# Output projection of a hybrid attention block: halves by kind of head, another order of the products, other banks

## The chip, the cores and the metric

The kernel runs on one core of a Trainium2 chip. The metric is the device time of one execution in microseconds (us); the median of several runs is compared.

## What is computed

One layer of a streaming encoder: a combined input projection, 16 heads of attention (8 stick-breaking, 8 forgetting), an output projection with a residual, a squared-ReLU MLP with a residual, a final norm. 512 tokens, width 2048, all in float32. The change touches the line with `w_out`:

```python
mixed = jnp.concatenate([head_rmsnorm(o_sb, g_out_sb[l]),
                         head_rmsnorm(o_fox, g_out_fox[l])], axis=-1)
x = x + jnp.einsum('bse,ed->bsd', mixed, w_out[l])

h2 = rmsnorm(x, g_mlp[l])
u = jax.nn.relu(jnp.einsum('bsd,df->bsf', h2, w_up[l]))
x = x + jnp.einsum('bsf,fd->bsd', u * u, w_down[l])
```

`mixed` has 16 heads of 128 columns: heads 0 to 7 are stick-breaking, 8 to 15 forgetting.

## The kernel before

Every float32 product is three fp32r matmuls on TensorE (`mm3`, lines 76 to 79): high by high, high by low, low by high. An operand is split by a cast on ScalarE (line 59, the high part) and a subtraction on VectorE (line 60, the low part).

The large products are Strassen-Winograd products: both operands are halved along both dimensions, 7 products of sums of quarters take the place of 8, and some products accumulate on others. The **output projection** (in the trace some 576 to 760 us) does this for two blocks of columns, `db` 0 and 1. Its left operand is `mixed`, halved along the tokens and along the heads: before, one half holds the even heads and the other the odd ones (`(m s)`: head 2m+s), so that a sum joins heads 2m and 2m+1, m = 0 to 7. `g_form(p, ...)` makes the split operand `G[p]` of product p for some m, in rooms of two halves (high and low) named by `ROOMS`. The row sums of `mixed` that the products need are made in place by VectorE (`a_source`, lines 1231 to 1239). The right operand, sums of quarters of `w_out`, comes ready from DRAM (`wraws`, `wsums`, `whigh`, made earlier by `WeightSums`) or is split on arrival.

A product is four pieces (`out_piece(p, db, m0)`, m0 = 0, 2, 4, 6; each two m). A piece is 12 matmuls of 128x512, so a product is 48. It accumulates in a PSUM tile of two banks, `[P, 2, NT]`; there are three, `accoa`, `accob`, `accoc`, called A, B, C. For db 0 the products 1, 6, 7, 4 follow one another in A (6 goes on where 1 ended, so 1 must be read out before 6 begins), 2 is in B, 5 and 3 in C; for db 1 A and B change places. The order of the products is 1, 2, 6, 5, 7, 3, 4.

Behind each product, `take(p, db)` adds the banks to a quarter of the residual x on VectorE (line 1453, one instruction of 128x1024, for product 4 two of 128x512); the quarters are loaded by `begin` (line 1447, 512 KB on SyncE's queue). When a quarter is whole, `turn_quarter` transposes it for the MLP: 8 transposes of 128x128 on TensorE (line 1460), two in a PSUM tile, copies with the norm's weight on ScalarE, and the quarter is written to DRAM. From the turned quarters `left_form` makes the left operands of the next stage. Pending left forms are taken up one by one behind pieces.

The heads end in the order forgetting 6, 7, 0 to 5, then stick-breaking 0 to 7. Stick-breaking 6 and 7 are the last; the pieces and sums with them come last in the stage's first products (m = 3 before).

The instructions of this stage are not ordered by hand: a scheduler orders each engine's queue from the program's dependences and its own durations; `issue_after` lines bind an instruction behind another. The weights' pieces rotate through three rooms (`hi_lo`), with a fourth (`px`) until product 5 of db 0.

Of the kernel before, what the change touches and what calls it, by code (L numbers as in the profile page):

```python
# [15 lines left out]
P = 128  # L16
# [21 lines left out]
def block_kernel(ctx, tc, x, g_attn, w_in, b_f, g_out_sb, g_out_fox, w_out, g_mlp, w_up, w_down, g_final, y):  # L38
# [676 lines left out]
    with tc.tile_pool(name="att", bufs=1, side="right", reuse_waits="tile") as at, \  # L715
# [259 lines left out]
        class WeightSums:  # L975
# [415 lines left out]
    A, B = (A, B), (B, A)  # L1391
    S_OF = xp.tile([P, NH, 2 * P], F32, tag="hr1", name="s12")
    out_rows = w_out.rearrange("(m s p) c -> s p m c", s=2, p=P)
# [12 lines left out]
    def out_piece(p, db, m0):  # L1406

        hi, lo = (w.rearrange("p (a b) -> p a b", a=2) for w in hi_lo(2 * NT))
        if db == 0 and p in (1, 2):
            begun_ = [sp.dma_start(w.bitcast(F32), wraws[p - 1][:, m0 // 2, i]) for i, w in enumerate((hi, lo))][1]  # L1410
        elif db == 0 and p == 6:
            begun_ = sp.dma_start(hi.bitcast(F32), whigh[:, m0 // 2])
            sp.dma_start(lo.bitcast(F32), wsums[:, m0 // 2, 3, db])
        else:
            raw = out_weights(p, db, m0)
            casts[0] = split(hi, lo, raw[0])
            begun_ = raw[1]
        ps = {2: B[db], 5: C, 3: C}.get(p, A[db])
        for t in range(2):
            ts = slice(t * P, (t + 1) * P)  # L1420
            for i in range(2):
                mm3(ps[:, t, :], G[p][0][:, m0 + i, ts], G[p][1][:, m0 + i, ts], hi[:, i, :], lo[:, i, :],
                    m0 + i == 4 and p in (1, 5, 2), m0 + i == 3)
        return begun_
# [15 lines left out]
    def begin(t, j, db):  # L1440

        if t + j + db == 0:

            quarter[t, j] = wp.tile([P, 2, NT], F32, tag="wraw", name="x2")
        else:
            quarter[t, j] = xp.tile([P, 2, NT], F32, tag="x2", name="x2", bufs=3)
        sp.dma_start(quarter[t, j], xq[:, 2 * t:2 * t + 2, (2 * j + db) * NT:(2 * j + db + 1) * NT])

    def take(p, db):
        q, ps = {1: ((0, 0), A[db]), 5: ((1, 1), C), 6: ((0, 1), A[db]), 2: ((0, 0), B[db]), 7: ((1, 1), A[db]),  # L1450
                 3: ((0, 1), C), 4: ((1, 0), A[db])}[p]
        for t in range(2) if p == 4 else [slice(0, 2)]:
            dve.tensor_tensor(quarter[q][:, t, :], quarter[q][:, t, :], ps[:, t, :], op=ALU.add)
# [40 lines left out]
    pending = []  # L1494
    for db in range(2):
        if db == 1:
            begin(0, 0, db)
        else:

            for p in (1, 2):  # L1500
                g_form(p, (4, 8), (0, 2), (2, 3))
            with tc.issue_after(last_heads[2].ins):
                for p in (4, 5):
                    g_form(p, (4, 8), (0, 2), (2, 3))
            more_parts.append(lambda: parts_at(px, "px"))
            out_piece(1, 0, 4)
            with tc.issue_after(last_heads[3].ins):
                out_piece(1, 0, 6)
            with tc.issue_after(last_heads[2].ins):
                with tc.issue_after(last_heads[0].ins):  # L1510
                    out_piece(1, 0, 0)
                    out_piece(2, 0, 4)
                with tc.issue_after(last_heads[1].ins):
                    out_piece(2, 0, 6)
                    out_piece(2, 0, 0)
            begin(0, 0, db)
            for p in (1, 2, 4, 5):
                g_form(p, (3, 4))
            g_form(6, (4, 6), (6, 8), (0, 2), (2, 4))
            last_heads[4] = lows[0]  # L1520
        for i, p in enumerate(G_ORDER):
            for m0 in (2,) if db == 0 and p in (1, 2) else (4, 6, 0, 2):
                ins = out_piece(p, db, m0)
                if pending:
# [3 lines left out]
                if (db or p in (3, 4)) and m0 in (6, 2) and first_loads:  # L1528
# [4 lines left out]
                if db == 0 and p in (6, 5, 7) and m0 == 2:  # L1533
# [3 lines left out]
                if db == 0 and p in (6, 5) and m0 != 4:  # L1537

                    with tc.issue_after(last_heads[4].ins):
                        g_form({6: 7, 5: 3}[p], {6: (4, 8), 0: (0, 2), 2: (2, 4)}[m0])  # L1540
# [6 lines left out]
            if db == 1 and p == 2:  # L1547
# [5 lines left out]
            if db == 1:  # L1553
                pending += [(q, 0, j) for q in A_ORDER[2 * i:2 * i + 2] for j in range(2)]
# [10 lines left out]
            if db == 1 and p == 3:  # L1565
                left_form(1, 1, 1)
                for j in range(2):
                    left_form(2, 1, j)
                for q in (4, 5, 6):
                    left_form(q, 1, 1)  # L1570
# [7 lines left out]
        else:  # L1578
            turn_quarter(1, 0, db)
# [583 lines left out]
```

## Time and profile before

| | us |
|---|---|
| median of 3 runs | 2004.07 |
| lowest, highest | 2003.90, 2004.32 |
| the profiled execution's span | 2002.0 |
| TensorE busy in it | 1993.2 |
| VectorE busy | 1745.6 |
| ScalarE busy | 1202.3 |

The span is measured from the first to the last instruction of the profiled execution; the runs' times are 2.07 longer by the median. PE is TensorE, DVE VectorE, ACT ScalarE, SP SyncE, whose queue issues the transfers. A matmul row shows a duration that overlaps with the next row's, since matmuls are pipelined; the pace is read from the starts.

### The profile page before, as it was taken

How to read it: one execution, taken by the hardware profiler on the slowest of the kernel's cores; microseconds unless marked ns; L12 is line 12 of the kernel's file. 1: busy time of each engine (PE TensorE's matmuls, PEld its weight loads, DVE VectorE, ACT ScalarE, POOL GpSimd, SP SyncE). 2: the span in 40 equal slices, each digit the busy share in tenths (PEclk: the TensorE clock that was granted, in tenths of full speed). 3: DMA queues.
4: the chain of work that ended last, by engine and by line, in shares of the span. 5: the costliest groups of instructions: out<-in, count | busy, mean ns of one | idle time of the engine just before them, and what ended most of it. 6: DMA issues, size and time to landing. Idle time of an engine off the chain costs nothing.

```text
span 2002.0 us, 27075 instructions
## 1 busy us (share of the span) xinstructions
PE 1993.2 (100%) x10288; PEld 1727.1 (86%) x10288; DVE 1745.6 (87%) x1997; ACT 1202.3 (60%) x1648; POOL 63.3 (3%) x73
## 2 busy tenths in 40 slices
PE   9999999999999999999999999999999999999998
PEld 9998888888898889888888888888888888888887
DVE  7886888888878678999999999998798888988896
ACT  7544766787765566767676776766543444344344
POOL 0000011010110000000000000000000000000003
PEclk9999999999999999999999999999999999999999
DMA  7417977777668962666766666666694674674642
GB/s 262 157 65 246 292 230 212 227 225 219 212 214 279 299 221 95 200 203 199 219 184 215 199 203 201 199 211 233 245 348 165 228 279 142 239 262 171 215 163 85
DMA packets 309570, 423.54 MB, mean 212 GB/s; under 512 B 49424, under 2 KB 205376, under 8 KB 302912
## 3 DMA queue, kind: packets, MB, share of 16 engines
q1 hardware_dynamic: 308688, 419.71, 63.9%
q10 hardware_dynamic: 752, 2.11, 0.3%
q8 instruction: 81, 1.33, 0.3%
q14 instruction: 49, 0.40, 0.1%
HBM read 315.45 MB, written 96.49 MB: 206 GB/s over the span
## 4 chain that ended last, share of the span: by engine, by line
PE 100%; DVE 0%; issue 0%; DVEq 0%; ACT 0%; ACTq 0%
PE psa L1313 11%; PE accd L79 8%; PE accd L77 8%; PE accd L78 8%; PE accq L77 6%; PE accq L78 6%; PE accq L79 6%; PE psa L1311 6%; PE psc L1313 5%; PE psc L1311 3%; PE psb L1313 3%; PE psb L1311 1%; PE m L79 1%; PE m L77 1%; PE m L78 1%; PE accoa L77 1%
## 5 line engine op out<-in xcount | busy, mean ns | idle before, releaser
L1949 ACT CAST wh<-wd 128x1024 fp32r<-128x1024 f32 x126 | 125.0, 998 | 168.2 <-PE accd L79 55.3
L1835 DVE TENSOR_TENSOR wl<-wu,wh 128x1024 fp32r<-128x1024 f32 x158 | 192.6, 1219 | 12.2 <-ACT wh L1829 12.0
L77 PE MATMUL accq<-hH,wh 128*128 128x512 f32 x512 | 200.3, 391 | 0.0
L78 PE MATMUL accq<-hL,wh 128*128 128x512 f32 x512 | 199.4, 389 | 0.0
L79 PE MATMUL accq<-hH,wl 128*128 128x512 f32 x512 | 199.4, 389 | 0.0
L1829 ACT CAST wh<-wu 128x1024 fp32r<-128x1024 f32 x158 | 167.6, 1061 | 44.0 <-issue 27.9
L1313 PE MATMUL psa<-f,wh 128*128 128x512 f32 x720 | 179.0, 391 | 0.0
L79 PE MATMUL accd<-wh,uf 128*128 128x512 f32 x436 | 169.6, 389 | 0.0
L78 PE MATMUL accd<-wl,uf 128*128 128x512 f32 x436 | 169.6, 389 | 0.0
L77 PE MATMUL accd<-wh,uf 128*128 128x512 f32 x436 | 169.5, 389 | 0.0
L1313 PEld LDWEIGHTS psa<-f,wh 128*128 128x128 f32 x720 | 132.3, 188 | 25.6
L1956 DVE TENSOR_TENSOR wl<-wd,wh 128x1024 fp32r<-128x1024 f32 x126 | 143.9, 1150 | 10.6 <-ACT wh L1949 10.6
L1949 ACT CAST wx<-wd 128x1024 fp32r<-128x1024 f32 (+1 forms) x82 | 80.8, 994 | 107.4 <-PE accd L79 43.6
L1670 DVE TENSOR_TENSOR m<-m,accd 128x1024 f32<-128x1024 f32 x84 | 102.1, 1216 | 47.9 <-PE accd L79 47.9
L79 PEld LDWEIGHTS accq<-hH,wl 128*128 128x128 f32 x512 | 96.1, 188 | 20.3
L77 PEld LDWEIGHTS accq<-hH,wh 128*128 128x128 f32 x512 | 96.2, 188 | 19.0
L78 PEld LDWEIGHTS accq<-hL,wh 128*128 128x128 f32 x512 | 96.2, 188 | 18.9
L77 PE MATMUL accd<-wx,uf 128*128 128x512 f32 x284 | 110.5, 389 | 0.0
L78 PE MATMUL accd<-wx,uf 128*128 128x512 f32 x284 | 110.5, 389 | 0.0
L79 PE MATMUL accd<-wx,uf 128*128 128x512 f32 x284 | 110.5, 389 | 0.0
L1311 PEld LDWEIGHTS psa<-f,wl 128*128 128x128 f32 x720 | 96.0, 191 | 5.4
L1311 PE MATMUL psa<-f,wl 128*128 128x256 f32 x720 | 98.3, 282 | 0.0
(464 smaller groups left out, 5120.5 us busy)
## 6 DMA issues: line engine op xcount, KB each, us to landing
wu<-in_w_up_dram SPq DMA_DIRECT2D x60, 1024.0 KB, 6.5
ufd<-st SPq DMA_DIRECT2D x98, 512.0 KB, 4.2
wd<-in_w_down_dram SPq DMA_DIRECT2D x48, 1024.0 KB, 8.4
uf<-ufd SPq DMA_DIRECT2D x42, 1024.0 KB, 7.5
wraw<-in_w_in_dram SPq DMA_DIRECT2D x68, 512.0 KB, 5.7
wo<-wsums SPq DMA_DIRECT2D x28, 512.0 KB, 4.7
q<-in_w_in_dram SPq DMA_DIRECT2D x32, 384.0 KB, 5.3
wd<-in_w_down_dram SPq DMA_DIRECT2D x16, 768.0 KB, 5.8
```

Of the source, the lines that this page charges most:

```text
L77: pe.matmul(out, sh, mh, start=first, stop=False, skip_group_check=True)
L78: pe.matmul(out, sh, ml, start=False, stop=False, skip_group_check=True)
L79: return pe.matmul(out, sl, mh, start=False, stop=last, skip_group_check=True)
L1311: ins = pe.matmul(ps[:, 2 * P:], lo[:, a, :], f_parts(p, a)[0], start=False, stop=last, skip_group_check=True)
L1313: ins = pe.matmul(ps, hi[:, a, :], f_both(p, a), start=a == PAIRS[0] and p in (1, 5), stop=last, skip_group_check=True)
L1670: dve.tensor_tensor(M[p][:, :, db, :], M[p][:, :, db, :], ps, op=ALU.add)
L1829: act.copy(rooms[k][0], srcs[k])
L1835: lows[0] = dve.tensor_tensor(lo, srcs.pop(k), hi.bitcast(F32), op=ALU.subtract)
L1949: act.copy(rooms[k + 3][0], srcs[k + 3])
L1956: dve.tensor_tensor(rooms[k + 2][1], srcs.pop(k + 2), rooms[k + 2][0].bitcast(F32), op=ALU.subtract)
```

## The change

Six things change in the output projection. (1) `mixed` and `w_out` are halved as `(s m)`: one half is the stick-breaking heads, the other the forgetting ones, and a sum joins heads m and m + 8. The last heads are then m = 6 and 7, and the pieces go in the order m0 = 0, 2, 4, 6. (2) Product 2 of db 0 and product 2 of db 1 come first; then product 1 of db 0, and 6, 5, 7, 3, 4; for db 1 1, 6, 5, 7, 3, 4. (3) The banks: product 2 in A (db 0) and B (db 1), the chain 1, 6, 7, 4 in C (db 0) and B (db 1), 5 and 3 in A (db 0) and C (db 1). (4) The residual quarter (0, 0) of db 1 is loaded at the start of the stage and kept, in the room `ROOMS[1]`, where the low half of product 2's operand lies before. (5) A turn is put on a list and made behind the first piece of the next product. (6) Left forms of db 1's partner operands are listed at other products.

```diff
@@ WeightSums.load
-                    src = w_out[(2 * self.m + s) * P:(2 * self.m + s + 1) * P].rearrange("p (j c) -> p j c", j=2)
+                    src = w_out[(s * NH + self.m) * P:(s * NH + self.m + 1) * P].rearrange("p (j c) -> p j c", j=2)
...
-    G_ORDER = (1, 2, 6, 5, 7, 3, 4)
+    G_ORDER = (1, 6, 5, 7, 3, 4)
     G = {p: [form.tile([P, NH, 2 * P], F32R, tag=ROOMS[2 * i + c], name=f"g{p}") for c in range(2)]
-         for i, p in enumerate(G_ORDER)}
+         for i, p in enumerate((2, 1, 6, 5, 7, 3, 4))}
...
-    A, B = (A, B), (B, A)
+    firsts, chains, sides = (A, B), (C, B), (A, C)
...
-            a_form(p, mixed[:, 2 * m0:2 * m1].rearrange("p (m s) n -> p m s n", s=2), [g[:, m0:m1, :] for g in G[p]])
+            a_form(p, mixed_halves[:, m0:m1], [g[:, m0:m1, :] for g in G[p]])
...
-        ps = {2: B[db], 5: C, 3: C}.get(p, A[db])
+        ps = {2: firsts[db], 5: sides[db], 3: sides[db]}.get(p, chains[db])
...
+        elif t + j == 0:
+            quarter[t, j] = form.tile([P, 2, NT], F32, tag=ROOMS[1], name="x2")
...
             g_form(2, (0, 4), (4, 8))
             g_form(1, (0, 4), (4, 6))
...
+                    for m0 in (0, 2, 4, 6):
+                        out_piece(2, 1, m0)
+                    for m0 in (0, 2, 4):
+                        out_piece(1, 0, m0)
+            begin(0, 0, 1)
+            kept = quarter[0, 0]
+            take(2, 1)
+            begin(0, 0, 0)
+            take(2, 0)
+            for p in (1, 5):
+                g_form(p, (6, 7), (7, 8))
+            g_form(6, (0, 4), (4, 6), (6, 8))
...
+        for p in G_ORDER:
+            for m0 in (6,) if db == 0 and p == 1 else (0, 2, 4, 6):
                 ins = out_piece(p, db, m0)
+                if m0 == 0 and to_turn:
+                    with tc.issue_after(ins.ins):
+                        turn_quarter(*to_turn.pop())
...
             if db == 1:
-                pending += [(q, 0, j) for q in A_ORDER[2 * i:2 * i + 2] for j in range(2)]
+                pending += [(q, 0, j) for q in {1: (4, 5, 6), 6: (2, 7), 5: (3,)}.get(p, ()) for j in range(2)]
...
-            if p in (2, 7, 3):
-                turn_quarter(*{2: (0, 0), 7: (1, 1), 3: (0, 1)}[p], db)
+            if p in (1, 7, 3):
+                to_turn.append(({1: (0, 0), 7: (1, 1), 3: (0, 1)}[p]) + (db,))
```

In the excerpts of the queues below a row is line, operation, output and inputs with the number of the tile, shape, and what the instruction waits for (queues of transfers, DVE, Activation, PE).

TensorE's queue of the kernel before, at the end of product 2 of db 0 and the start of product 6:

```order
L77 MATMUL accob_5600<-wh_5767,g2_5565 128x512
L78 MATMUL accob_5600<-wl_5768,g2_5565 128x512
L79 MATMUL accob_5600<-wh_5767,g2_5566 128x512
L77 MATMUL accoa_5599<-wx_5800,g6_5567 128x512 [waits DMAHW0_49,DVE_49,Activation_49]
L78 MATMUL accoa_5599<-wx_5800,g6_5567 128x512 [waits DMAHW1_49]
L79 MATMUL accoa_5599<-wx_5800,g6_5568 128x512 [waits DVE_49]
```

The same of the kernel after, at the end of product 1 of db 0 and the start of product 6:

```order
L77 MATMUL accoc_5601<-wh_5830,g1_5565 128x512
L78 MATMUL accoc_5601<-wl_5831,g1_5565 128x512
L79 MATMUL accoc_5601<-wh_5830,g1_5566 128x512
L77 MATMUL accoc_5601<-wx_5847,g6_5567 128x512 [waits DMAHW5_49,DVE_49,Activation_49]
L78 MATMUL accoc_5601<-wx_5847,g6_5567 128x512 [waits DMAHW6_49]
L79 MATMUL accoc_5601<-wx_5847,g6_5568 128x512
```

Before, product 6 in accoa begins behind product 2 in accob; after, it begins in the bank in which the matmul ahead of it, the last of product 1, is.

VectorE's queue before, in the same place (x2 is a residual quarter, g1 to g7 the operands' low halves, ph a head's norm, wx a weight's split):

```order
L969 SCALAR_TENSOR_TENSOR mixed_1750<-os_last_5528,g_rest_78,ph_5530 128x512 [waits DVE_49]
L60 TENSOR_TENSOR g2_5566<-mixed_1750,g2_5565 128x256 [waits Activation_49]
L60 TENSOR_TENSOR g4_5576<-mixed_1750,g4_5575 128x256 [waits Activation_49]
L1453 TENSOR_TENSOR x2_5727<-x2_5727,accoa_5599 128x1024 [waits DMAHW5_49,PE_49]
L60 TENSOR_TENSOR g6_5568<-mixed_1750,g6_5567 128x512 [waits Activation_49]
L1233 TENSOR_TENSOR mixed_1750<-mixed_1750 128x256 [waits DVE_49]
L60 TENSOR_TENSOR g6_5568<-mixed_1750,g6_5567 128x512 [waits Activation_49] x2
L1453 TENSOR_TENSOR x2_5727<-x2_5727,accob_5600 128x1024 [waits DVE_49,PE_49]
L60 TENSOR_TENSOR g5_5570<-mixed_1750,g5_5569 128x256 [waits Activation_49]
L1235 TENSOR_TENSOR mixed_1750<-mixed_1750 128x2x256 [waits DVE_49]
L60 TENSOR_TENSOR wx_5877<-wo_5878,wx_5877 128x1024 [waits DMAHW6_49,DMAHW1_49,DMAHW7_49,DMAHW0_49,Activation_49]
```

After, up to the addition of product 1 of db 0, the last row:

```order
L60 TENSOR_TENSOR g6_5568<-mixed_1750,g6_5567 128x1024 [waits PE_49,Activation_49]
L60 TENSOR_TENSOR g6_5568<-mixed_1750,g6_5567 128x512 [waits Activation_49]
L60 TENSOR_TENSOR g5_5570<-mixed_1750,g5_5569 128x256 [waits Activation_49]
L1233 TENSOR_TENSOR mixed_1750<-mixed_1750 128x2x256 [waits DVE_49]
L1454 TENSOR_TENSOR x2_5805<-x2_5805,accob_5600 128x1024 [waits DMAHW3_49,PE_49]
L60 TENSOR_TENSOR g6_5568<-mixed_1750,g6_5567 128x512 [waits Activation_49]
L1235 TENSOR_TENSOR mixed_1750<-mixed_1750 128x4x256
L1235 TENSOR_TENSOR mixed_1750<-mixed_1750 128x2x256 x2
L1237 TENSOR_TENSOR mixed_1750<-mixed_1750 128x4x256
L1237 TENSOR_TENSOR mixed_1750<-mixed_1750 128x2x256 x2
L60 TENSOR_TENSOR g7_5572<-mixed_1750,g7_5571 128x1024 [waits Activation_49]
L1454 TENSOR_TENSOR x2_5808<-x2_5808,accoc_5601 128x1024 [waits PE_49]
```

The addition of accob, product 2 of db 1, to the kept quarter x2_5805 stands there, ahead of the sums for g7 and of the addition of accoc.

SyncE's queue before, at the weights of products 1, 2 and 6 of db 0:

```order
L1410 DMA wl_5751<-wraws1_93 128x1024 [waits DMAHW4_49,PE_49]
L1410 DMA wh_5750<-wraws1_93 128x1024 [waits DMAHW5_49,PE_49]
L1410 DMA wl_5768<-wraws2_94 128x1024 [waits DMAHW6_49,DMAHW0_49,PE_49]
L1410 DMA wh_5767<-wraws2_94 128x1024 [waits DMAHW7_49,DMAHW1_49,PE_49]
L1412 DMA wx_5800<-whigh_92 128x1024 [waits PE_49]
L1413 DMA wx_5800<-wsums_86 128x1024
L1413 DMA wl_5816<-wsums_86 128x1024 [waits DMAHW2_49,PE_49]
```

After:

```order
L1409 DMA wl_5790<-wraws1_93 128x1024 [waits PE_49]
L1409 DMA wh_5789<-wraws1_93 128x1024 [waits DMAHW1_49,PE_49]
L1409 DMA wl_5831<-wraws1_93 128x1024 [waits DMAHW2_49,PE_49]
L1448 DMA x2_5805<-in_x_dram 128x2x512 [waits DMAHW3_49,PE_49]
L1409 DMA wh_5830<-wraws1_93 128x1024 [waits DMAHW4_49]
L1411 DMA wx_5847<-whigh_92 128x1024 [waits DMAHW5_49,PE_49]
L1412 DMA wx_5847<-wsums_86 128x1024 [waits DMAHW6_49]
```

The load of the kept quarter stands between the two halves of the last weights of product 1, and waits for PE.

## Rows read from the trace of the kernel before

**Rows 1.** The page: busy time of engines, granted clock, chain of work.

```profile
PE 1993.2 (100%) x10288; PEld 1727.1 (86%) x10288; DVE 1745.6 (87%) x1997; ACT 1202.3 (60%) x1648; POOL 63.3 (3%) x73
...
PE 100%; DVE 0%; issue 0%; DVEq 0%; ACT 0%; ACTq 0%
```

**Rows 2.** PE's waits: line waited for, us in total, times, longest.

```profile
PE vx L305 <- DVE still L301: 1.6, 1, 1.6
```

**Rows 3.** Windows: length, busy us of PE, PEld, DVE, ACT, POOL; clock, DMA.

```profile
620.00:770.00 150.00, 150.00 (x757) 127.40 (x756) 113.31 (x122) 91.22 (x145) 0.00 (x0) 1.00 0.71 231
```

**Rows 4.** Timeline of PE (start, us, line, out<-in), where the bank changes.

```profile
660.96 0.39 PE L77 MATMUL accoc<-wh,g 128*128 128x512 f32 x1
...
661.41 0.39 PE L79 MATMUL accoc<-wh,g 128*128 128x512 f32 x1
661.64 0.39 PE L77 MATMUL accoa<-wh,g 128*128 128x512 f32 x1
```

**Rows 5.** Timeline of PE at a turn.

```profile
655.27 0.40 PE L77 MATMUL accoc<-wh,g 128*128 128x512 f32 x1
655.51 1.04 PE L1460 MATMUL tr<-ident,x 128*128 128x128 f32 x8
...
656.61 0.39 PE L79 MATMUL accoc<-wh,g 128*128 128x512 f32 x1
```

**Rows 6.** Timeline of DVE at two takes; in brackets idle time before, and its releaser.

```profile
661.84 1.22 DVE L1453 TENSOR_TENSOR x<-x,accoc 128x1024 f32<-128x1024 f32 x1 [0.41 <-PE accoc L79]
...
685.40 1.22 DVE L1453 TENSOR_TENSOR x<-x,accob 128x1024 f32<-128x1024 f32 x1 [0.18 <-PE accob L79]
```

**Rows 7.** Timeline of PE at the first piece of product 2.

```profile
605.24 0.39 PE L77 MATMUL accob<-wx,g 128*128 128x512 f32 x1
```

**Rows 8.** Timeline of DVE: the first sum g4, and instructions of each size in a row.

```profile
595.09 2.15 DVE L60 TENSOR_TENSOR g<-mixed,g 128x1024 fp32r<-128x1024 f32 x3
...
603.43 0.68 DVE L1235 TENSOR_TENSOR mixed<-mixed 128x512 f32<-128x512 f32 x1
604.03 0.41 DVE L60 TENSOR_TENSOR g<-mixed,g 128x256 fp32r<-128x256 f32 x1
604.37 1.28 DVE L1235 TENSOR_TENSOR mixed<-mixed 128x512 f32<-128x512 f32 x2
...
607.10 0.69 DVE L967 TENSOR_TENSOR n<-n,ra 128x512 f32<-128x512 f32 x1
607.83 0.69 DVE L968 SCALAR_TENSOR_TENSOR n<-n,ra 128x512 f32<-128x512 f32 x1
...
631.16 1.21 DVE L60 TENSOR_TENSOR g<-mixed,g 128x1024 fp32r<-128x1024 f32 x1
632.30 1.22 DVE L60 TENSOR_TENSOR wl<-wo,wh 128x1024 fp32r<-128x1024 f32 x1
```

**Rows 9.** Timeline of DVE where it stood idle in this stretch, and at product 1's take.

```profile
606.38 0.69 DVE L966 SCALAR_TENSOR_TENSOR n<-ssq,ra 128x512 f32<-128x512 f32 x1 [0.72 <-ACT ra L961]
...
612.83 0.76 DVE L60 TENSOR_TENSOR g<-mixed,g 128x256 fp32r<-128x256 f32 x2 [0.47 <-ACT g L59]
614.28 1.22 DVE L1453 TENSOR_TENSOR x<-x,accoa 128x1024 f32<-128x1024 f32 x1 [0.70 <-PE accoa L79]
```

**Rows 10.** The residual's tiles (x) in 560 to 770: their transfers, issue to landing.

```profile
DMA to landing us min/median/max: 4.3/5.2/7.8
```

**Rows 11.** PE's last matmul, and windows behind them (clock behind POOL's column).

```profile
1994.47 0.28 PE L79 MATMUL acce<-ws,us 128*128 128x256 f32 x1
...
1996.50:1997.00 0.50, 0.00 (x0) 0.00 (x0) 0.50 (x3) 0.41 (x2) 0.00 (x0) 1.00 0.00 0
1997.00:1997.50 0.50, 0.00 (x0) 0.00 (x0) 0.50 (x2) 0.50 (x2) 0.00 (x0) 0.53 0.00 0
```

**Rows 12.** Timeline of PE at the start of the kernel.

```profile
1.58 1.65 PE L305 MATMUL vx<-still 128*128 128x256 f32 x6 [1.58 <-DVE still L301]
...
7.62 0.40 PE L311 MATMUL vz<-wl,hH 128*128 128x264 f32 x2
```

More of the change, by code (lines that the diff above doesn't have):

```diff
@@ L1422, in out_piece @@
                 mm3(ps[:, t, :], G[p][0][:, m0 + i, ts], G[p][1][:, m0 + i, ts], hi[:, i, :], lo[:, i, :],
-                    m0 + i == 4 and p in (1, 5, 2), m0 + i == 3)
+                    m0 + i == 0 and p in (1, 5, 2), m0 + i == NH - 1)
         return begun_
@@ L1492, in left_form @@
         a_form(p, hr[db][j], [F[p][db][:, 2 * j:2 * j + 2, c, :] for c in range(2)])
-    pending = []
+    pending, kept, to_turn = [], None, []
     for db in range(2):
         if db == 1:
-            begin(0, 0, db)
-        else:
-            for p in (1, 2):
-                g_form(p, (4, 8), (0, 2), (2, 3))
+            quarter[0, 0] = kept
+            pending += [(1, 0, j) for j in (1, 0)]
+        else:
+            g_form(2, (0, 4), (4, 8))
+            g_form(1, (0, 4), (4, 6))
             with tc.issue_after(last_heads[2].ins):
-                for p in (4, 5):
-                    g_form(p, (4, 8), (0, 2), (2, 3))
+                g_form(4, (0, 4), (4, 8))
+                g_form(5, (0, 4), (4, 6))
@@ L1520, in block_kernel @@
+            g_form(6, (0, 4), (4, 6), (6, 8))
             last_heads[4] = lows[0]
-        for i, p in enumerate(G_ORDER):
-            for m0 in (2,) if db == 0 and p in (1, 2) else (4, 6, 0, 2):
+        for p in G_ORDER:
+            for m0 in (6,) if db == 0 and p == 1 else (0, 2, 4, 6):
                 ins = out_piece(p, db, m0)
+                if m0 == 0 and to_turn:
+                    with tc.issue_after(ins.ins):
+                        turn_quarter(*to_turn.pop())
+                    if db == 1 and p == 4:
+                        left_form(1, 1, 1)
+                        for j in range(2):
+                            left_form(2, 1, j)
+                        for q in (4, 5, 6):
+                            left_form(q, 1, 1)
@@ L1527, in block_kernel @@
                         left_form(*pending.pop(0))
-                if (db or p in (3, 4)) and m0 in (6, 2) and first_loads:
+                if (db or p in (3, 4)) and m0 in (2, 6) and first_loads:
                     with tc.issue_after(ins.ins):
@@ L1532, in block_kernel @@
                         units[u].load(k, a)
-                if db == 0 and p in (6, 5, 7) and m0 == 2:
+                if db == 0 and p in (6, 5, 7) and m0 == 6:
                     with tc.issue_after(ins.ins):
                         begin(*{6: (0, 1), 5: (1, 1), 7: (1, 0)}[p], db)
-                if db == 0 and p in (6, 5) and m0 != 4:
+                if db == 0 and p in (6, 5) and m0 != 0:
                     with tc.issue_after(last_heads[4].ins):
-                        g_form({6: 7, 5: 3}[p], {6: (4, 8), 0: (0, 2), 2: (2, 4)}[m0])
+                        g_form({6: 7, 5: 3}[p], {2: (0, 4), 4: (4, 6), 6: (6, 8)}[m0])
             if db == 0 and p == 5:
@@ L1546, in block_kernel @@
                 units += [Unit(0), Unit(1)]
-            if db == 1 and p == 2:
+            if db == 1 and p == 1:
                 begin(0, 1, db)
@@ L1560, in block_kernel @@
                     take_squares()
-            if p in (2, 7, 3):
-                turn_quarter(*{2: (0, 0), 7: (1, 1), 3: (0, 1)}[p], db)
+            if p in (1, 7, 3):
+                to_turn.append(({1: (0, 0), 7: (1, 1), 3: (0, 1)}[p]) + (db,))
             if db == 1 and p == 6:
                 left_form(1, 1, 0)
[L1565 to L1570, printed above, removed]
         if db == 1:
@@ L1578, in block_kernel @@
         else:
-            turn_quarter(1, 0, db)
+            to_turn.append((1, 0, db))
     ops.close()
```

19 lines of the change are left out of this document (7 added, 12 removed).

## The prediction

> **What bounds the kernel now.** I read the page first. TensorE is busy for 1993.2 us of a span of 2002.0, and the chain of work that ended last is put down to PE at 100% [rows 1]. The list of waits then has one entry for PE, 1.6 us at the very start [rows 2], and in a stretch that holds most of the output projection (620 to 770 us) PE is busy in 150.00 of 150 us and at full clock, while VectorE has 113.31 [rows 3]. So PE alone sets the end. A change that leaves the number of matmuls as it is can win only gaps of PE, and it loses whatever new wait it puts into PE's queue. The order confirms that the products are the same: 14 products (7 for each column block db) of 48 matmuls 128x512.
>
> What can be won? A matmul follows the last every 0.2266 us, also where the bank changes [rows 4]. The only places in the stage where this pace breaks are the turns of the residual: 8 transposes between two matmuls, as the one at 655.51 [rows 5]. A transpose has a quarter of the columns, so 0.057 us by the same pace, and 8 of them 0.45. From the matmul ahead (655.27) to the second behind (656.61) there are 1.34 us, of which 0.45 + 2 x 0.227 are due: a loss of 0.43. Eight turns lose 3.5. **A gain is bounded by about 3.5 us**, and only if all transposes leave the place between matmuls, which the change does not do.
>
> **The change, part by part.**
>
> *Turns behind a piece.* Before, the turns stood 25 matmuls into a following product already (so by the order; the one at 655.51 is in accoc's product [rows 5]). Now they are hung behind the first piece (12 matmuls) of the next product, and the scheduler puts most of them where they stood. Value 0; bounds -0.3 to 0.2, half of one turn's loss to either side, rounded.
>
> *Halves by kind of head and product 2 first.* The sums of heads are now head k plus or minus head k+8. The pieces that need the heads finished last (stick-breaking 6 and 7) are the last of each product, so product 1 of db 0 now needs them only in its last piece, at 624.3 by the count below, where before that product was whole and read out at 614.28 [rows 9]. Both product 2s (96 matmuls) run without them. I looked whether that cover is needed: PE waits for nothing there now, so its worth is 0. What it costs is in the queues. Four weight splits of 128x1024 on VectorE and one take (the addition of a bank to the residual) for product 2 of db 1 come ahead of db 0's other products instead of behind them, into the stretch where VectorE still has the last heads' norms and the sums g6 and g7.
>
> *Banks.* Product 6 continues to accumulate on product 1's bank (it needs 1+6), so its first matmul must wait until VectorE has read product 1 out. Before, product 2 stood between the two, in another bank: 48 x 0.2266 = 10.9 us in which the take was hidden. Now 6 follows 1 in the same bank with nothing between, in both column blocks; the order shows a wait for DVE on that first matmul, and the take itself as one instruction for both banks. This is a new wait on the only engine that matters. Its bare price: the last matmul of a product starts at 661.41, the take at 661.84 (0.43 later, after 0.41 of idle time, so VectorE was ready), and lasts 1.22 [rows 6]. With about 0.1 for the signal back (no row shows it; 0 to 0.3), less the 0.23 that the next matmul would take anyway: 0.43 + 1.22 + 0.1 - 0.23 = **1.5 us** for each of the two, if VectorE stands ready.
>
> *Is VectorE ready at the first one?* PE first. The first piece of product 2 begins at 605.24 before [rows 7]; up to there PE has done 48 matmuls of the first two products (36 of product 1, 12 of 2; in the new order all 48 of product 2), so in the new one product 2 of db 1 begins there. Behind it come 96 matmuls until product 1 ends: last matmul 605.24 + 95 x 0.2266 = 626.77, take possible at 627.2, product 6 due at 627.0. Now VectorE. From the first sum g4 (595.09 [rows 8]) up to the take the new order has 15 instructions of 128x1024, 12 of 128x512, 6 of 128x256 and 8 of the norm chain. One follows another by 1.14, 0.60, 0.35 and 0.71 [rows 8]: 17.1 + 7.2 + 2.1 + 5.7 = 32.1 us, so it reaches the take at 627.2 if it never waits. There is no slack, and every wait of VectorE before this point lengthens PE's stall. Such waits:
> - for ScalarE's casts. Before, VectorE lost 0.72 and 0.47 at two such places [rows 9]. In the new order two stand out: a sum behind the rooms it is written to, and g6, queued on ScalarE behind the cast for the last head. I take 0.3 + 0.75 = 1.05; bounds 0.3 to 1.6.
> - for the residual quarter of db 1. Its load goes to the room in which the low half of product 2's operand lies, so SyncE may issue it only when PE has ended product 2 of db 1: 605.24 + 48 x 0.2266 = 616.1, with drain and issue 616.9 to 617.2. The transfers of x in this stretch, its loads and its writes, take 4.3 to 7.8 us from issue to landing, 5.2 by the median [rows 10]; I use 4.5 to 6.1, some 0.8 around it: landed 621.6 to 623.2. VectorE reaches the addition that needs it 6.4 us of work and that addition's 1.14 ahead of the take, at 619.6, with the waits above about 621.0. Wait 0.6 to 2.2; queued behind it are a sum g6, six sums for the next products, g7 and the take for which PE stands. The load also stands ahead of product 1's last weights on SyncE, which would land near 622 and are wanted at 624.3, and so cost nothing.
> - 0.2 for the take of db 0's product 2, which waits for PE.
>
> Together 1.8 to 3.4. The **first stall** is then 1.5 + (1.8 to 3.4) = 3.3 to 4.9; I take 4.1.
>
> *The second stall* (db 1, seven products later, near 700). The take of 685.40 waited 0.18 for PE and so was reached at 685.22 [rows 6]; VectorE arrives just in time there. 1.5; bounds 1.4 to 2.2.
>
> *VectorE in db 1's products 6 and 5* has more splits and left forms ahead of the weights' due times; by my count the margins are 0.8, 0.25 and 0.2 us at three pieces. 0.2; bounds 0 to 0.6.
>
> **Sum:** 4.1 + 1.5 + 0.2 = +5.8 on a span of 2002.0. The median of the runs, 2004.07, is 2.07 above the profiled span, which I carry over: 2002.0 + 5.8 + 2.07 = **2009.9**. By the bounds (3.3 + 1.4 + 0 - 0.3 = 4.4 and 4.9 + 2.2 + 0.6 + 0.2 = 7.9) this case reaches from 2008.5 to 2012.0.
>
> **The rivals.**
>
> *The clock falls in the first stall.* [...] PE then resumes at half pace: at the start of the kernel six matmuls 128x256 last 1.65 us, or 0.27 each, against 0.113 by the pace of [rows 4] for half the columns; two of 128x264 in 0.40 at 7.62 are about full pace again [rows 12]. Some 5 us at half pace lose about 2.5, a part of that 1.7. Time 2009.9 + 1.7 to 2.5 = 2011.6 to 2012.4, with the stall's spread of 0.8 up to 2013.2. Against it: one place at the end shows the fall, and a PE that merely stands between two full-rate stretches is not in this trace. [...]
>
> *VectorE is ready after all (the side that is not slower).* If the casts cost nothing and the quarter lands before VectorE comes to it, it reaches the take at 627.2, and only the two bare waits stay: 2 x 1.5 = +3.0, that is 2007.1. It decides from the point where 1.8 us of waits vanish. For it: my count adds up the queue in the order printed, and a duration 2% shorter over 32 us gives back 0.6; before, VectorE had idle time in this stretch [rows 9]. Against it: the load's issue is tied to PE, and 4.3 us is the quickest transfer [rows 10].
>
> *The wait is not there.* If product 6's first matmul waited only for an older event, or the take were early, the sum would be near 0 to +1: 2004 to 2005. The order speaks against it, since the bank's chain needs the readout.
>
> *A gain.* Turn gaps closed and no stall: at best 2000.5. Nothing in the order shows it.
>
> **How the numbers follow.** Forecast 0.42 (2009.9). Clock falls 0.31 (2011.6 to 2013.2). VectorE ready 0.17 (2007.1). Wait not there 0.07 (2004.5). Gain 0.03. From below, leaving out the last two (0.10) brings the low end to 2006.7, 0.4 under the third; the high end takes in the clock's case to 2013.2 and leaves out under 0.1. 0.2% of 2004.07, about what a measurement of this kernel can tell from no change, is 4.0 us: 2000.1 to 2008.1. Faster: the 0.03 of a gain. Same: 0.17 + 0.07, less a little of the former's upper end: 0.22. Slower: 0.75.
>
> **What would show it.** Right: in the list of waits of the changed kernel two entries of PE for DVE, of 3 to 5 us near 627 and about 1.5 near 700, both at the first matmul of product 6 and behind the take; VectorE busy without idle from about 621 up to it, with an idle of 0.6 to 2.2 before the addition of the kept quarter, released by a DMA. A granted clock under 1.00 behind 627 is the second case. Two stalls of 1.5 are the third. Wrong would be: no wait of PE at a first matmul of product 6; a stall elsewhere (the weights of product 1's last piece, the last heads); a PE stall of over 6 us; or turns that lose much less than 0.43 each.

## The result, and the profile after

The changed kernel takes 2011.79 us (median of 5 runs, 2011.61 to 2012.32) against 2004.06 (5 runs, 2003.90 to 2004.32): 7.73 us more, a ratio of 1.0039 with a 95% interval of 1.0027 to 1.0052. It is slower, by 0.4%. The time lies in the predicted range (2006.7 to 2013.2), but the forecast's own case (2009.9) is not the one that occurred: it is the second, in which the clock falls.

The list of PE's waits in the profile after (line waited for, us in total, times, longest), which answers to [rows 2], has two new entries, both at the first matmul of product 6, which follows product 1 in the same bank with the read-out between them (a hand-over, below). "Issue" on the first means that the profile names no releaser; the rows of VectorE below name it.

```profile
PE accoc L77 <- issue: 4.3, 1, 4.3
...
PE accob L77 <- DVE x L1454: 1.4, 1, 1.4
```

The timeline of PE after at these two places and at a short wait ahead of the first, where product 1's last weights are late (start, us, line, out<-in, in brackets the idle time before and its releaser):

```profile
624.09 0.39 PE L79 MATMUL accoc<-wh,g 128*128 128x512 f32 x1
624.56 0.47 PE L77 MATMUL accoc<-wh,g 128*128 128x512 f32 x1
...
627.16 0.39 PE L79 MATMUL accoc<-wh,g 128*128 128x512 f32 x1
631.88 0.77 PE L77 MATMUL accoc<-wx,g 128*128 128x512 f32 x1 [4.33 <-issue]
632.44 0.63 PE L78 MATMUL accoc<-wx,g 128*128 128x512 f32 x1
632.87 0.63 PE L79 MATMUL accoc<-wx,g 128*128 128x512 f32 x1
...
635.33 0.39 PE L79 MATMUL accoc<-wx,g 128*128 128x512 f32 x1
...
702.23 0.39 PE L79 MATMUL accob<-wh,g 128*128 128x512 f32 x1
704.02 0.47 PE L77 MATMUL accob<-wh,g 128*128 128x512 f32 x1 [1.41 <-DVE x L1454]
```

Product 1 ends with the matmul at 627.16, product 6 begins at 631.88 instead of 627.39: 4.49 us. Of its first eight matmuls six are 0.43 apart where [rows 4] has 0.2266; from 635.33 on the pace is 0.23 to 0.24 again. Set against the due time those eight lose 1.6. The second hand-over, 702.23 to 704.02, loses 1.56. The late weights at 624.56 lose 0.33, the matmul behind included (this trace names no releaser there; two of the runs below name the weights' transfer). Together 4.49 + 1.6 + 1.56 + 0.33 = 8.0; the span grew from 2002.0 to 2010.1, by 8.1. Nothing else in the stage breaks the pace but the eight turns, which cost what they did.

VectorE after, from the addition of product 2 of db 1 to that of product 1 of db 0 (same columns):

```profile
617.77 2.16 DVE L60 TENSOR_TENSOR g<-mixed,g 128x1024 fp32r<-128x1024 f32 x3 [0.53 <-ACT g L59]
619.97 0.69 DVE L1233 TENSOR_TENSOR mixed<-mixed 128x512 f32<-128x512 f32 x1
623.01 1.22 DVE L1454 TENSOR_TENSOR x<-x,accob 128x1024 f32<-128x1024 f32 x1 [2.35 <-DMA x<-in_x_dram]
624.15 0.68 DVE L60 TENSOR_TENSOR g<-mixed,g 128x512 fp32r<-128x512 f32 x1
624.75 2.42 DVE L1235 TENSOR_TENSOR mixed<-mixed 128x1024 f32<-128x1024 f32 x3
627.09 2.42 DVE L1237 TENSOR_TENSOR mixed<-mixed 128x1024 f32<-128x1024 f32 x3
629.43 1.22 DVE L60 TENSOR_TENSOR g<-mixed,g 128x1024 fp32r<-128x1024 f32 x1
630.56 1.21 DVE L1454 TENSOR_TENSOR x<-x,accoc 128x1024 f32<-128x1024 f32 x1
```

The reader is to see three things. VectorE stands for 2.35 us for the load of the kept quarter. From 623.01 it works without a pause for 7.6 us, on things that PE does not need yet, while PE stands from 627.4. The addition that PE needs comes last, at 630.56, and 1.3 us later PE goes on.

Windows of after (length, busy us of PE, PEld, DVE, ACT, POOL, then the granted clock, DMA share, GB/s):

```profile
616.50:623.00 6.50, 6.50 (x31) 5.37 (x30) 3.58 (x6) 2.68 (x5) 0.00 (x0) 1.00 0.99 357
627.00:631.00 4.00, 0.55 (x3) 0.12 (x1) 4.00 (x6) 3.17 (x6) 0.00 (x0) 1.00 1.03 422
631.00:635.00 4.00, 3.12 (x7) 2.48 (x8) 4.00 (x6) 0.00 (x0) 0.00 (x0) 0.60 1.03 413
```

The first window is that of the kept quarter's load. While PE stands, from 627 to 631, the granted clock is 1.00; in the four us in which PE resumes it is 0.60 as a mean, 0.50 for four fifths of them.

### The profile page after: what moved, and what is told of

Read it like the earlier page. It is cut to its first block, busy times and chain, and to the rows that moved or that the text cites. A ratio compares the mean times of both kernels' runs of the same rounds, so it can differ in the third digit from the quotient of the medians.

```text
span 2010.1 us, 27073 instructions
## 1 busy us (share of the span) xinstructions
PE 1995.4 (99%) x10288; PEld 1728.1 (86%) x10288; DVE 1745.3 (87%) x1991; ACT 1202.2 (60%) x1643; POOL 64.1 (3%) x73
## 4 chain that ended last, share of the span: by engine, by line
PE 99%; DVE 0%; DMA 0%; issue 0%; ACT 0%; DVEq 0%; SPq 0%; ACTq 0%
PE psa L1311 11%; PE accd L79 8%; PE accd L77 8%; PE accd L78 8%; PE accq L77 6%; PE accq L78 6%; PE accq L79 6%; PE psa L1309 6%; PE psc L1311 5%; PE psc L1309 3%; PE psb L1311 3%; PE psb L1309 1%; PE m L79 1%; PE m L77 1%; PE m L78 1%; PE accoc L77 1%
```

## The experiments

Each kernel is the changed one, or where it says so the one before, with the edit shown. "Before" is measured again beside each set, with medians of 2003.84 to 2004.00; ratios are to it.

**What lengthens the first stall.** Two kernels take away what stands ahead of the addition that PE needs. In the first, product 2 of db 1 is added to the kept quarter behind it:

```diff
-            take(2, 1)
...
+            taken = take(p, db)
+            if db == 0 and p == 1:
...
+                with tc.issue_after(taken.ins):
+                    take(2, 1)
```

> As the changed kernel, but VectorE adds product 2 of db 1 to the kept quarter only behind the addition of product 1 of db 0, so nothing queued ahead of that addition waits for the kept quarter's load. Theory (the first stall is a bare bank hand-over lengthened by the load's wait of 2.35 us and the 1.14 us of the addition behind it, and a clock that falls because the stall is long): the addition of product 1 starts about 0.4 us behind the last matmul of product 1, the first stall is 1.6 us as the second, the clock stays at 1.00, 2004.07 + 2 x 1.56 + 0.3 = 2007.5. Rival (VectorE has too much work in this stretch whatever it waits for): the stall stays over 3 us, 2009.5 or more. Rival on the clock (it falls at any stall): 2009.

Measured 2009.84 (ratio 1.0029, 1.0020 to 1.0039). VectorE around the addition, and PE behind it:

```profile
627.51 2.42 DVE L60 TENSOR_TENSOR g<-mixed,g 128x1024 fp32r<-128x1024 f32 x3
629.85 1.21 DVE L1454 TENSOR_TENSOR x<-x,accoc 128x1024 f32<-128x1024 f32 x1
```

```profile
628.41 0.39 PE L79 MATMUL accoc<-wh,g 128*128 128x512 f32 x1
631.16 0.47 PE L77 MATMUL accoc<-wx,g 128*128 128x512 f32 x1 [2.37 <-issue]
```

The wait for the load is gone, but the scheduler used the time for all three splits of g7 where the changed kernel has one (629.43 there): 1.2 us more ahead of the addition. The stall is 2.52 instead of 4.49, with 0.7 of late weights ahead of it. My number was missed because the expectation held the rest of the queue fixed. In the profiled run the clock stays at 1.00 (628 to 636); the ten times lie from 2008.84 to 2011.64, five up to 2009.54 and five from 2010.14 on. The mean granted clock is 0.998 in all five of the upper ones and 0.999 in four of the lower, so a clock that falls at 2.5 us in some executions is likely; only one has a trace, so this is not shown.

In the second the six sums and the splits behind them are held back:

```diff
                     with tc.issue_after(last_heads[4].ins):
                         g_form({6: 7, 5: 3}[p], {2: (0, 4), 4: (4, 6), 6: (6, 8)}[m0])
...
-            take(p, db)
+            taken = take(p, db)
+            if db == 0 and p == 1:
+                last_heads[4] = taken
```

> As the changed kernel, but the sums for products 7 and 3 (six additions and the splits, 6.5 us on VectorE ahead of the addition of product 1 of db 0) may come only behind that addition; the addition to the kept quarter with its wait for the load stays ahead of it. Theory: the load's wait matters only through what is queued behind it; VectorE takes product 1 out at once, first stall 1.6, no fall of the clock, 2007.5. Rival (the load itself ends last): a stall of over 2.5 us. Rival (the sums are then late for product 7): a new stall of 1 us or more some 22 us later, 2008.5 to 2010.

Measured 2007.64 (1.0016, 1.0007 to 1.0026), as expected. VectorE at the two additions, and PE at the first hand-over:

```profile
622.34 1.22 DVE L1454 TENSOR_TENSOR x<-x,accob 128x1024 f32<-128x1024 f32 x1 [2.08 <-DMA x<-in_x_dram]
...
627.18 1.22 DVE L1454 TENSOR_TENSOR x<-x,accoc 128x1024 f32<-128x1024 f32 x1 [3.02 <-PE accoc L79]
```

```profile
626.75 0.39 PE L79 MATMUL accoc<-wh,g 128*128 128x512 f32 x1
628.50 0.47 PE L77 MATMUL accoc<-wx,g 128*128 128x512 f32 x1 [1.36 <-issue]
```

VectorE still waits 2.08 for the load, and now 3.02 for PE: it is ready, and the stall is the bare 1.52. So the load's wait hurts only through the queue behind it, and 4.1 of the 7.7 us that the change cost go when the sums for products 7 and 3 are held back. Product 7 shows no wait.

**The price of one hand-over.** Product 1 is added in two halves, one for each bank:

```diff
-        for t in range(2) if p == 4 else [slice(0, 2)]:
+        for t in range(2) if p in (1, 4) else [slice(0, 2)]:
```

> As the changed kernel, but product 1 is added to the residual in two instructions of 128x512, one for each bank. Theory (product 6 waits for the readout of the bank that it writes): its first matmuls need the first bank alone, so each of the two stalls is 0.55 shorter (1.0 and 3.9), the clock still falls in the first: 2011.79 - 1.1 = 2010.7. If 3.9 us no longer lets the clock fall: 2009.1. Rival (the wait is for the whole tile): both stalls as they were, 2011.8.

Measured 2011.97 (1.0038, 1.0024 to 1.0053): the rival. PE and VectorE at the first hand-over:

```profile
626.77 0.39 PE L79 MATMUL accoc<-wh,g 128*128 128x512 f32 x1
630.91 0.69 PE L1461 MATMUL tr<-ident,x 128*128 128x128 f32 x2 [3.75 <-DVE x L1454]
631.55 0.77 PE L77 MATMUL accoc<-wx,g 128*128 128x512 f32 x1
```

```profile
630.17 1.28 DVE L1454 TENSOR_TENSOR x<-x,accoc 128x512 f32<-128x512 f32 x2
```

The stalls of 3.91 and 1.03 that the theory asked for are there, but what ends them is not product 6. The scheduler put two transposes of the quarter's turn into each hand-over; they read the first half of the sum and start behind it. Product 6 begins behind the second half, 0.10 after its end (630.17 + 1.28 = 631.45), as it begins 0.10 after the end of the whole read-out in the changed kernel (630.56 + 1.21 = 631.77, and 631.88); in the second hand-over it is 0.06 behind the second half. Counted to its first matmul the hand-overs take 4.55 and 1.53, where the whole read-out has 4.49 and 1.56. So in these kernels PE waits for the read-out of both banks, and halving it wins nothing by itself. The clock is at half for longer on top:

```profile
631.00:635.00 4.00, 4.00 (x10) 3.00 (x11) 3.99 (x6) 0.00 (x0) 0.00 (x0) 0.50 1.04 416
635.00:637.00 2.00, 2.00 (x6) 1.41 (x6) 0.00 (x0) 0.00 (x0) 0.00 (x0) 0.50 0.39 156
```

It is at 0.50 through 636.8, for 12 matmuls and the transposes ahead of them instead of 8 matmuls; on the 12 that costs 2.5 where the changed kernel pays 1.6. Against it stand no late weights (0.33 in the changed kernel) and turns of which two transposes lie in the stall.

All three edits together:

> As the changed kernel, with three edits together: the addition to the kept quarter and the sums for products 7 and 3 come only behind the addition of product 1 of db 0, and product 1 is added in two instructions of 128x512. Theory: two stalls of 1.03 us, the price of the second stall with half takes, 0.3 us of late weights ahead of the first, no fall of the clock: 2004.0 + 2.1 + 0.3 = 2006.4. Rival (the sums held back are late for product 7, or ScalarE's turn of the first quarter is): 2007.5 or more.

Measured 2007.20 (1.0017, 1.0008 to 1.0026), 0.8 more than expected. PE and VectorE:

```profile
628.39 0.39 PE L79 MATMUL accoc<-wh,g 128*128 128x512 f32 x1
629.56 0.44 PE L1462 MATMUL tr<-ident,x 128*128 128x128 f32 x2 [0.78 <-DVE x L1454]
630.21 0.47 PE L77 MATMUL accoc<-wx,g 128*128 128x512 f32 x1 [0.20 <-issue]
```

```profile
628.82 1.28 DVE L1454 TENSOR_TENSOR x<-x,accoc 128x512 f32<-128x512 f32 x2 [5.62 <-PE accoc L79]
```

It is the same here, and plainer: VectorE has stood ready for 5.62, the two transposes are done, and PE still stands 0.20 until the second half has ended (630.10). Up to the transposes the stalls are 0.94 and 1.16; up to product 6 they are 1.59 and 1.67. With late weights of 0.4 that makes 3.7, of which 0.2 are the transposes' own columns: near the 3.2 that the median lies above the kernel before. The expectation had counted on hand-overs of 1.03. The profiled execution (2008.35) lies above the median for another reason: it is 1.2 late in all that follows the start (its last head's products begin at 598.12, 596.91 before), and that is lost in the first 12 us, where from 8.5 to 10 it has 9 matmuls and the kernel before 14. The edit does not touch that stretch. In the profiled run of the turns alone, whose edit does not touch it either, the last head's products begin at 598.57.

**The clock.** Matmuls that nobody reads, into a bank that is free then, fill the first stall (`last_mm` is the last matmul of the piece):

```diff
...
+                if db == 0 and p == 1:
+                    with tc.issue_after(last_mm[0].ins):
+                        for _ in range(18):
+                            pe.matmul(B[:, 0, :], G[1][0][:, 0, :P], G[1][0][:, 0:2, :], start=True, stop=True, skip_group_check=True)
```

> As the changed kernel, but 18 matmuls of 128x512 that nobody reads stand between product 1 and product 6 of db 0, into a bank that is free then: 4.1 us of work for TensorE inside the first stall. Theory (TensorE waits there for VectorE alone, and the clock falls because TensorE stands idle): product 6 begins as late as before, at about 631.9, but at full clock, 1.6 us less: 2010.2. Rival (the clock fell for another reason, or its price is not 1.6): 2011.8. Rival (the stall has room for less than 4.1 us): above 2012.

Measured 2010.54 (1.0032, 1.0021 to 1.0044; six executions, 2009.72 to 2012.46). PE and the clock:

```profile
627.49 4.24 PE L1536 MATMUL accob<-g 128*128 128x512 f32 x18
631.71 0.47 PE L77 MATMUL accoc<-wx,g 128*128 128x512 f32 x1
```

```profile
631.00:635.00 4.00, 4.00 (x21) 3.04 (x20) 4.00 (x6) 0.26 (x1) 0.00 (x0) 1.00 1.03 415
```

Product 6 begins as late as in the changed kernel, at 631.71, and runs at full clock. The profiled spans differ by 1.8 (2010.1, 2008.3), the medians by 1.25. That the fall came from PE standing idle is shown; its price is 1.3 to 1.8 by these two differences, and 1.6 by the rows of the changed kernel.

**The parts alone, on the kernel before.** The turns behind a piece:

```diff
+                if m0 == 4 and to_turn:
+                    with tc.issue_after(ins.ins):
+                        turn_quarter(*to_turn.pop())
...
             if p in (2, 7, 3):
-                turn_quarter(*{2: (0, 0), 7: (1, 1), 3: (0, 1)}[p], db)
+                to_turn.append(({2: (0, 0), 7: (1, 1), 3: (0, 1)}[p]) + (db,))
```

> As the kernel before, with the turns alone put behind the first piece of the next product; halves, order of the products and banks as before. Theory: eight turns cost TensorE 0.43 each wherever they stand between matmuls, 2004.0 (same). Rival (a turn that comes earlier makes left forms earlier or pushes splits of weights on VectorE and ScalarE back): 2005 or more. Rival (a gain from whole turns): 2003.5 or less.

Measured 2003.94 beside 2003.96 (1.0000, 0.9991 to 1.0009): nothing, as predicted. The halves by kind of head:

```diff
-    out_rows = w_out.rearrange("(m s p) c -> s p m c", s=2, p=P)
+    out_rows = w_out.rearrange("(s m p) c -> s p m c", s=2, p=P)
...
-            for m0 in (2,) if db == 0 and p in (1, 2) else (4, 6, 0, 2):
+            for m0 in (6,) if db == 0 and p in (1, 2) else (0, 2, 4, 6):
...
```

> As the kernel before, with the halves by kind of head alone (pieces in the order m0 = 0, 2, 4, 6, the last heads in the last pieces); order of the products, banks and turns as before. Theory: TensorE waits for nothing there before, and the instructions are the same, 2004.0 (same). Rival (the halves carry part of the loss, through the sums of the last heads): 2005 or more. Rival (they carry a gain that the stalls hide): 2003 or less.

Measured 2005.21 (1.0006, 0.9997 to 1.0015). The median is 1.25 above, inside the interval of no change, but the trace has one clear wait:

```profile
616.63 0.39 PE L79 MATMUL accoa<-wh,g 128*128 128x512 f32 x1
618.38 0.47 PE L77 MATMUL accoa<-wx,g 128*128 128x512 f32 x1 [1.36 <-issue]
```

It is the same hand-over. The scheduler put the last piece of product 2 ahead of product 1's, so that product 6 follows product 1 in accoa. I then bound product 2's last piece behind product 1:

```diff
+            if db == 0 and p == 2 and m0 == 6:
+                behind.enter_context(tc.issue_after(last_mm[0].ins))
```

> As the kernel with the halves alone, but the last piece of product 2 of db 0 may come only behind the last matmul of product 1, so that product 2's piece stands between product 1 and product 6 again. Theory (the halves by themselves cost nothing; the 1.5 us there came from product 6 following product 1 in one bank): no wait of TensorE at product 6, 2004.0, about 1.2 below the kernel with the halves alone (2005.21). Rival (the last heads are late for product 1's last piece in the new halves): a wait of 0.5 to 2 us at that piece, 2004.5 to 2006.

Measured 2006.12 (1.0012, 1.0003 to 1.0020), above the kernel before and not below the halves alone: the rival. The hand-over is gone and another wait has its place:

```profile
611.55 0.39 PE L79 MATMUL accoa<-wh,g 128*128 128x512 f32 x1
613.81 0.50 PE L77 MATMUL accoa<-wh,g 128*128 128x512 f32 x1 [1.87 <-ACT g L59]
```

Product 1's last piece now needs heads 6 and 7, the last two, and stands 2.0 us for their split. My theory that the halves cost nothing falls: with them, product 1 must not end as early as it did, and either the hand-over or the last heads are paid.

**Other places for the hand-over.** The products in the order 1, 5, 6, 3, 7, 4:

```diff
-    G_ORDER = (1, 6, 5, 7, 3, 4)
+    G_ORDER = (1, 5, 6, 3, 7, 4)
```

> As the changed kernel, but the products after 2 come in the order 1, 5, 6, 3, 7, 4: product 5 in another bank stands between 1 and 6, product 3 between 6 and 7, and the one hand-over inside a bank is now from 7 to 4. Theory (each column block pays one hand-over inside a bank, and the price is bare where VectorE has little queued): no wait at product 6, one of 1.5 us at the first matmul of product 4 in each block, no fall of the clock: 2004.0 + 3.1 = 2007.1. Rival (product 5's weights, which VectorE must split, are late when it comes straight behind product 1 while VectorE still has the last heads' sums): a stall of 1 to 4 us there, 2008 to 2011.

Measured 2010.24 (1.0033, 1.0021 to 1.0045), in the range of the rival. The left forms of product 2 were made from a sum that product 3 had overwritten, which changes values but not the work; the next kernel lists them in the right order.

> The order 1, 5, 6, 3, 7, 4 again, now with the left forms of products 2 and 7 listed behind product 5 and that of 3 behind product 6, so that in db 1 they are made in the order 5, 6, 2, 7, 3. Theory: three waits as seen in the run of that order: 1.0 at product 5's weights, 1.56 and 2.1 at the first matmul of product 4, no fall of the clock: 2004.0 + 4.7 = 2008.7; the early part of that run was 1.2 late, which is not of the change. Rival (that 1.2 belongs to the order): 2010.2.

Measured 2009.27 (1.0028, 1.0017 to 1.0038). PE's waits in it:

```profile
PE accob L77 <- DVE x L1454: 2.3, 1, 2.3
...
PE accoc L77 <- DVE x L1454: 1.4, 1, 1.4
PE accoa L78 <- DVE wl L60: 0.8, 1, 0.8
PE accoa L77 <- ACT wh L59: 0.3, 1, 0.3
```

The hand-over moved from product 6 to product 4, as expected, bare in db 0 (1.56 with the matmul's start) and 2.49 in db 1, where VectorE is busy; product 5, straight behind product 1, waits 1.5 for its weights. The clock fell behind the wait of 2.3 in db 1 (0.50 from 748.5 to 751.5), in this execution, the longest of the eight (2011.73); two more, of 2010.51 and 2010.69, have a mean granted clock of 0.998, and the other five lie from 2009.00 to 2009.30. The time is between the expectation (2008.7) and its rival (2010.2).

**A separator in each hand-over**, that is matmuls of another product in another bank. Product 2 of db 1 is cut: two pieces ahead of product 1, one between 1 and 6 of db 0, one between 1 and 6 of db 1. With it go the kept quarter, which is loaded at db 1's start again, and the sums for products 7 and 3, which stay behind the addition of product 1.

```diff
-    firsts, chains, sides = (A, B), (C, B), (A, C)
+    firsts, chains, sides = (A, B), (C, A), (A, C)
...
+            if p == 1:
+                out_piece(2, 1, 6 if db else 4, last_mm[0])     # behind product 1's last matmul
```

> As the changed kernel (halves by kind of head, product 2 of db 0 first, turns behind a piece), but product 2 of db 1 is cut: two of its pieces stand ahead of product 1 of db 0, one between product 1 and product 6 of db 0, one between product 1 and product 6 of db 1; the chain of db 1 is in accoa, product 2 of db 1 alone in accob, the quarter of db 1 is loaded at db 1's start, and the sums for products 7 and 3 come behind the addition of product 1 of db 0. Theory (the whole loss is the two hand-overs inside a bank and what lengthens the first): 12 matmuls, 2.7 us, stand in each hand-over, which needs 1.5; TensorE waits at neither product 6, the last heads have 618.8 to be ready: 2004.0 to 2004.5, no measurable change from the kernel before. Rival (the last heads or the additions are still late): a wait of 1 to 2 us near 619 or at product 6, 2005 to 2006. Rival (db 1's left forms, begun later again, are late for the next stage): a wait behind 760, 2006 or more.

Measured 2010.55 (1.0032, 1.0019 to 1.0044). PE at the first hand-over, and at the end of the stage:

```profile
622.42 0.39 PE L79 MATMUL accoc<-wh,g 128*128 128x512 f32 x1
622.65 0.39 PE L77 MATMUL accob<-wh,g 128*128 128x512 f32 x1
...
625.37 0.39 PE L77 MATMUL accoc<-wh,g 128*128 128x512 f32 x1
```

```profile
754.71 0.39 PE L79 MATMUL accoa<-wh,g 128*128 128x512 f32 x1
758.39 0.51 PE L77 MATMUL psa<-f,wh 128*128 128x256 f32 x1 [3.29 <-DVE x L1457]
```

Both hand-overs of product 6 are without a wait (there are two short waits elsewhere, of 0.58 at product 1's start and 0.69 for weights). But I had put the last chain into accoa, in whose place the next stage writes first (psa), and made a third hand-over there, of 3.45 us, with the clock at half behind it (0.57 as a mean from 758 to 762). The next run shows that it is the bank. With the chain in accob as in the kernel before:

```diff
-    firsts, chains, sides = (A, B), (C, A), (A, C)
+    firsts, chains, sides = (B, A), (C, B), (B, C)
```

> The same cut of product 2 of db 1, with other banks: the chain of db 1 is in accob, product 2 of db 1 in accoa, product 2 of db 0 and products 5 and 3 of db 0 in accob, of db 1 in accoc. In the run ahead TensorE waited at neither product 6, but 3.5 us at the first matmul of the next stage, which writes the bank that product 4 of db 1 had just used, and its clock fell there. Theory (that wait is a third hand-over inside a bank): with product 4 of db 1 in accob, which the next stage does not write first, the wait is gone, only the 0.6 and 0.7 us of late weights stay: 2004.0 + 1.3 = 2005.3. Rival (the left forms or the last quarter are late themselves): the wait stays, 2010.

Measured 2007.05 (1.0015, 1.0006 to 1.0025). PE has no wait left in the whole stage, and one ahead of it:

```profile
585.70 0.28 PE L79 MATMUL accv<-wh,hL 128*128 128x256 f32 x1
587.51 1.31 PE L885 MATMUL pt<-ident,w 128*128 128x128 f32 x10 [1.54 <-POOL w L786]
```

In the kernel before and in the changed one the first 12 matmuls of the projection stand in this place, in accoa. Here the first product is in accob, and its first matmul comes only at 596.59, behind the last attention products; that accob is not free earlier is the likely reason and not shown. This costs 1.7 there and some 0.9 in the short gaps between 591.6 and 594.5. No arrangement that I ran is faster than the kernel before.

## Why the prediction was right, and where it was off

**What bounds the kernel** held: with TensorE at 100%, the matmuls unchanged and no gap to win, only new waits could decide, and they did. Faster was excluded rightly.

**The hand-over inside the bank** held in place and price: 1.5 predicted, 1.56 (second stall), 1.52 (sums held back), 1.52 (halves alone) measured, and 1.53 to 1.67 with the read-out in two halves. For the signal back, 0.1 in the sum, the prediction had no row; product 6 begins 0.10 behind the read-out's end in the first stall and 0.15 in the second.

**VectorE's lateness** held as a mechanism; the sizes were off both ways. The load's wait was 2.35, above the bound of 2.2: it was issued at 616.53, 0.37 behind the first matmul of the next product (616.16), where the prediction had 0.8 to 1.1 for drain and issue, which no row shows; its addition began 6.5 us later, where I had taken up to 6.1 for the landing. The share of the DMA engines was 0.99 there (357 GB/s from 616.5 to 623), which is the likely reason and not shown. The casts cost 0.26 and 0.53 instead of 1.05, product 2's take nothing. Together the waits are 3.14, where the 4.1 holds 2.6; PE ended product 1 0.39 later than I had counted (627.16, not 626.77), which took most of that back. So 4.49 against 4.1, inside 3.3 to 4.9, is closer than its parts, and that is luck. What I did not see is that the order was at fault more than the load: 5.8 us of sums and a split, wanted 20 us later, stood between the load and the addition, and held back they cost nothing.

**Late weights** at product 1's last piece: I said that they cost nothing; they cost 0.33, a small case of the "stall elsewhere" that I had named as a sign of being wrong.

**Turns** 0 predicted, 0 measured (2003.94 against 2003.96). **The second stall** 1.5 against 1.56; product 6's and 5's weights in db 1, 0.2, cost nothing.

**The clock** was the step that failed: its fall is the case that occurred, and I had put it second, at 0.31. I had the row of a fall, to 0.53, some 2.3 us behind the last matmul [rows 11] and a stall of 4.1. Against it I set an estimate of mine, that a stall of this size can pass without a fall; no row showed that. In all five runs of the changed kernel the mean granted clock was 0.997 or 0.998, and in ten runs of the kernel with the sums held back, with stalls of 1.52 and 1.57, 0.999 (0.999 alone does not exclude a fall: the profiled execution of the corrected order has one, and 0.999). In the traces the clock fell with stalls of 4.49 (the changed kernel), 3.91 (half takes) and 3.45 (product 2 cut, first banks), once with 2.49 (the corrected order) and not with 2.52 (the kept quarter behind), 2.08 (the order before its correction) and 2.03 (product 1 first); with 1.7 and less it never did. So at 4.5 it was the likeliest case; at 2.5 both are seen, so there the length of the stall alone does not decide. Its price, 1.7 to 2.5 predicted, was 1.3 to 1.8 by the filler and 1.6 by the rows; 2.5 appeared with half takes. The 5 us at half pace in that price were an estimate from the start of the kernel [rows 12], where the granted clock is 1.00 (1.5 to 4 us); behind the first stall it is 0.50 for some 3.4 us, 631.8 to 635.2.

**What lies around the span**: I carried over 2.07, the distance of the shown median from the profiled span. The executions with their own span listed have 1.7, so the profiled one of before was itself some 0.4 faster than the median. With the four terms of the result: 2002.0 + 8.0 + 1.7 = 2011.7, measured 2011.79.

**The halves**: I gave the cover of the last heads a worth of 0 since PE waited for nothing before. Right for the old halves, wrong for the new: there, with product 1 ending early, PE stands 2.0 us for the last heads. Taking product 2 of both blocks first, which needs the forgetting heads alone, pays for that, and takes away the separator in doing so.

## What to carry to other kernels

Two products that accumulate in one bank with a read-out between them made PE wait here, 1.52 to 1.57 us where VectorE stood ready; another product's matmuls between them took that wait away (12 matmuls, 2.7 us, were enough; that some 1.5 us would do is an estimate from the wait). A read-out in two halves did not shorten the wait here. When an order of products is changed, list the bank hand-overs of the whole stage and of the next stage's first bank, since a hand-over that was cured in one place turned up in two others here (product 4's, and the next stage's first). Then look at what stands ahead of the read-out on the engine that makes it: work with a late due time is bound behind it first, which here won back 4.1 of 7.7 us by itself. A stall of several microseconds was paid twice here, once as idle time and once at half clock (4.49 and 1.6).

## What was not expected of the hardware

The clock fell after PE had gone on, in one run. In the kernel with the corrected order PE stands 2.34 us up to 747.30, runs some 1.1 us at full pace, and then at half:

```profile
747.00:748.50 1.50, 1.20 (x5) 1.06 (x6) 1.29 (x2) 0.00 (x0) 0.00 (x0) 0.95 0.36 150
748.50:751.50 3.00, 3.00 (x8) 2.27 (x8) 0.00 (x0) 0.00 (x0) 0.00 (x0) 0.50 0.24 100
```

So matmuls at half pace need not stand right behind a gap; that this gap brought the fall is likely by the filler's run and not shown. And a shorter stall had a longer time at half clock: 12 matmuls and the transposes ahead of them behind 3.91 us, 8 matmuls behind 4.49.
